# The gates of the last 64 dense tokens kept in SBUF, and eight e-tiles of activations under way in the dense loop

## The chip, the core and the metric

The kernel runs on one core of a Trainium2 chip. The core has a matrix engine (PE, with weight loads shown as PEld), a vector engine (DVE), an activation engine (ACT), GpSimd (POOL) and a queue engine (SP) that issues most transfers. The metric is device time of one execution in microseconds (us), lower is better.

## What is computed

One layer of an encoder block for 512 tokens of width 1024: attention in two branches, then a PEER feed-forward part with 16384 single-neuron experts. The change lies in the PEER part, of which this is the core:

```python
s1 = jnp.einsum('thc,hnc->thn', q[:, :, 0], sub_keys[:, 0])
s2 = jnp.einsum('thc,hnc->thn', q[:, :, 1], sub_keys[:, 1])
...                                   # top 16 of each half, top 16 of the sums
eidx = e1 * PEER_N_KEYS + e2          # 8 heads x 16 experts per token
gate = jax.nn.softmax(top, axis=-1)
act = jax.nn.gelu(jnp.einsum('td,thkd->thk', xc, expert_u[eidx]))
return jnp.einsum('thk,thkd->td', gate * act, expert_v[eidx])
```

## The kernel before

The 512 tokens are split. For 128 of them (block a = 0) the chosen experts are gathered one slot at a time: a job gathers one expert row per token by an indirect transfer on POOL (tile `gat`, 4 buffers, L1058) and DVE reduces it (`gscr`, L1064, for the rows of `expert_u`; `acc`, L1076, for those of `expert_v`). There are 264 jobs, spread by program order over the rest of the kernel.

For the other 384 tokens (ND = 384, blocks DT = 1, 2, 3) the part is computed densely. The experts are 128 e-tiles of 128. For each e-tile:

- `gelu_s` (L870 to L879) loads the tile of `expert_u` (512 KB, tile `raw`), splits it into two float32r parts (`whi` on ACT, L91; `wlo` on DVE, L92), runs 24 matmuls of 384 columns into `pj` (L86 to L88) and writes the Gelu to an `am` tile of 128 x 384. For the first NS = 96 e-tiles this is done ahead (`run_ahead`) and `am` is stored to the DRAM tensor `gls`; for the last 32 it is done in the dense loop. Here "u tile" means one such e-tile.
- The dense loop multiplies `am` by the gates (L1201), splits the product into `ah` and `al`, loads and splits the tile of `expert_v` ("v tile", 512 KB) and runs 18 matmuls of 512 columns into `y` (L1220).

The gates are made dense before the loop, 4 tokens at a time: DVE writes one-hot tiles `oh` (L1125) and `og` (L1130), PE multiplies them into `pg` (L1137), ACT copies `pg` into a `stage` tile that holds 32 tokens (L1139). After each 32 tokens four transfers store the stage to the DRAM tensors `gd` (L1146); there are 12 such groups. In the loop, `gch` (L1164) loads the gates of 8 e-tiles, all 12 groups at once, into one of two buffers.

The e-tiles run in chunks of 8. The order of the chunks is 12, 0, 1, 2, 13, 3, 4, 5, 14, 6, 7, 8, 15, 9, 10, 11; chunks 12 to 15 need `expert_u` in the loop, the others load `am` from `gls`. `stage_s` prepares the e-tile that is LEAD tiles ahead.

What sets the order of the work: a scheduler places each engine's instructions in a fixed order when the kernel is built. Engines run their own order and wait where data or a buffer is missing; SP issues its transfers in order too. The tiles of `expert_u` and `expert_v` share one pool (`w4`, L794): 3 `raw` buffers, 5 `whi` and 5 `wlo`. So the transfer of tile k waits for the split of tile k-3, and the split of tile k for the matmuls of tile k-5.

Of the kernel before, what the change touches and what calls it, by code (L numbers as in the profile page):

```python
# [15 lines left out]
F32 = mybir.dt.float32  # L16
# [6 lines left out]
OP = mybir.AluOpType  # L23
# [872 lines left out]
def peer(K, A, out):  # L896
    nc, cst, gen, Pool = K.nc, K.cst, K.gen, K.Pool
    small, f2, mm3, split, ident = K.small, K.f2, K.mm3, K.split, K.ident
    h2tok = K.h2tok
    gd, gls = A['gd'], A['gls']  # L900
    ND, NS = 384, 96
    RT, OB, SB, J0, GB = 8, 3, 2, 48, 4
    DT = (1, 2, 3)
    pss = Pool("pss", space=PSUM, side="right")
    pe_ = Pool("pse", space=PSUM)
# [1 line left out]
    pa = Pool("am")  # L907

    def pmat():
        return pss.tile([128, 512], F32, name="pj", bufs=2)  # L910
# [4 lines left out]
    def ptr():  # L915
        return pe_.tile([128, 512], F32, name="pt", bufs=2)

    def pg():
        return pe_.tile([128, 512], F32, name="pg", bufs=2)
# [40 lines left out]

    def run_ahead():
        if K.ahead < NS:
            K.run_ahead(pmat(), pa.tile([128, ND], F32, name="am", bufs=4), nc.vector)

    tk = K.wk = Pool("tk")
    wq = A['w_query'].rearrange("(k p) n -> p k n", p=128)
# [54 lines left out]
    def slots(p, a):  # L1021
        rb = ranks(p, a).rearrange("p h f k -> p (h f) k")

        eq = p.tile([128, 16, 16, 16], BF, name="eq", bufs=1)
        for r in range(16):
            nc.vector.scalar_tensor_tensor(eq[:, r], rb, float(r), ib[:, a, :, r, None].to_broadcast([128, 16, 16]),
                                           op0=OP.is_equal, op1=OP.mult)
        ev = eq.rearrange("p r s k -> p r (s k)")
        n = 8
        while n > 1:  # L1030
            nc.vector.tensor_tensor(ev[:, 0:n], ev[:, 0:n], ev[:, n:2 * n], op=OP.add)
            n //= 2
        ef = p.tile([128, 2, 128], F32, name="ef", bufs=2)
        nc.vector.tensor_tensor(ef.rearrange("p f (h k) -> p h f k", k=16), eq[:, 0].rearrange("p (h f) k -> p h f k", f=2),
                                eq[:, 1].rearrange("p (h f) k -> p h f k", f=2), op=OP.add)
        e = [ef[:, f, :] for f in range(2)]
        g = p.tile([128, 8, 16], F32, name="gate", bufs=2)
        nc.vector.tensor_tensor(g, top[:, a], top[:, a, :, 0:1].to_broadcast([128, 8, 16]), op=OP.subtract)
        nc.scalar.activation(g, g, AF.Exp)
        z = small(8)  # L1040
        nc.vector.tensor_reduce(out=z, in_=g, op=OP.add, axis=AX)
        rz = small(8)
        nc.vector.reciprocal(rz, z)
        nc.vector.tensor_tensor(g, g, rz[:, :, None].to_broadcast([128, 8, 16]), op=OP.mult)
        return e[0], e[1], g.rearrange("p h k -> p (h k)")


    g0 = Pool("g0", side="right")
# [38 lines left out]
    def run_jobs(done):  # L1087
        while jobs and njobs - len(jobs) < done:
            jobs.pop(0)()


    gt = K.wk = Pool("gates")
    T = 4

    GS = 16384.0
    iota = gt.tile([128, 128, T], HF, name="iota")
    nc.vector.tensor_copy(iota, ioti[:, :, None].to_broadcast([128, 128, T]))
    e1, e2, g = slots(gt, 0)
    nc.vector.scalar_tensor_tensor(eidx, e1, 128.0, e2, op0=OP.mult, op1=OP.add)
    nc.vector.tensor_copy(gate0, g)  # L1100
    for b, a in enumerate(DT):
        tr = []
        for n, t in enumerate(slots(gt, a)):
            p = ptr()
            nc.tensor.transpose(p[:, :128], t, ident)
            s = gt.tile([128, 128], HF if n < 2 else F32, name=f"sT{n}", bufs=2)
            nc.scalar.activation(s, p[:, :128], AF.Copy, scale=1.0 if n < 2 else GS)
            tr.append(s)
        gT = tr[2]
        gp = []  # L1110
        for i in range(2):
            q = gt.tile([128, 128], HF, name=f"gp{i}", bufs=2)
            nc.vector.tensor_copy(q, gT)
            if i == 0:
                nc.vector.tensor_tensor(gT, gT, q, op=OP.subtract)
            gp.append(q)
        for t0 in range(0, 128, T):
            ts = slice(t0, t0 + T)
            tb = t0 % 32
            if tb == 0:  # L1120
                st = gt.tile([128, 128, 32], F32, name="stage", bufs=SB)
            oh = []
            for i in range(2):
                o = gt.tile([128, 128, T], HF, name=f"oh{i}", bufs=OB)
                nc.vector.tensor_tensor(o, tr[i][:, None, ts].to_broadcast([128, 128, T]), iota, op=OP.is_equal)  # L1125
                oh.append(o)
            pcs = []
            for i in range(2):
                o = gt.tile([128, T, 128], HF, name=f"og{i}", bufs=OB)
                nc.vector.tensor_tensor(  # L1130
                    o, oh[0].rearrange("p e t -> p t e"), gp[i][:, ts, None].to_broadcast([128, T, 128]), op=OP.mult)
                pcs.append(o)
            for q in range(0, T, 4):
                p = pg()
                for j in range(4):
                    for i in range(2):
                        nc.tensor.matmul(p[:, j * 128:j * 128 + 128], oh[1][:, :, q + j], pcs[i][:, q + j, :],  # L1137
                                         start=i == 0, stop=i == 1)
                nc.scalar.activation(st[:, :, tb + q:tb + q + 4].rearrange("p e t -> p t e"),  # L1139
                                     p.rearrange("p (t e) -> p t e", t=4), AF.Copy, scale=1 / GS)  # L1140
            if t0 % 16 == RT:
                run_ahead()
            run_jobs(J0 * (128 * b + t0 + T) // 384)
            if tb == 28:
                for c in range(4):
                    nc.sync.dma_start(gd[c][4 * b + t0 // 32].rearrange("c p e t -> p c (e t)"),  # L1146
                                      st[:, 32 * c:32 * c + 32, :].rearrange("p (c e) t -> p c (e t)", e=8))
    while K.ahead < NS:
        run_ahead()
# [8 lines left out]
    lp = Pool("main")  # L1158
    gch, ams = {}, {}

    def stage_s(e):
        if e % 8 == 0:
            gch[e // 8] = lp.tile([128, 12, 8, 32], F32, name="gch", bufs=2)
            nc.sync.dma_start(gch[e // 8].rearrange("p h e t -> p h (e t)"),  # L1164
                              gd[e // 32][:, e // 8 % 4].rearrange("h p e t -> p h (e t)"))
        am = ams[e] = pa.tile([128, ND], F32, name="am", bufs=4)
        if e < NS:
            nc.sync.dma_start(am, gls[e])
        else:
            gelu_s(e, pmat(), am, nc.vector)  # L1170
# [16 lines left out]
            (nc.scalar if n else nc.sync).dma_start(ov[:, a, ns], y)  # L1187

    PR = (0, 1)
    LEAD = 4  # L1190
    for e in order[:LEAD]:
        stage_s(e)
    pool_order = K.tc.manual_schedule(engines={mybir.EngineType.Pool})
# [2 lines left out]
    for n_, e in enumerate(order):  # L1196
        if n_ + LEAD < 128:
            stage_s(order[n_ + LEAD])
        am = ams.pop(e)
        amv = am.rearrange("p (h t) -> p h t", t=32)  # L1200
        nc.vector.tensor_tensor(amv, amv, gch[e // 8][:, :, e % 8, :], op=OP.mult)  # L1201
        ah = lp.tile([128, ND], F32R, name="ah", bufs=2)
        al = lp.tile([128, ND], F32R, name="al", bufs=2)
        split(ah, al, am)
        raw, vh, vl = w4(v[e])
        split(vh, vl, raw, nc.vector)
        if n_ == 126:
            run_jobs(njobs)
            for a in range(4):
                xr[a] = g0.tile([128, 1024], F32, name="gat", bufs=GB)  # L1210
                nc.sync.dma_start(xr[a], A['x1d'][:, a, :])
            residual(0)
        for b in range(3):
            bs = slice(b * 128, b * 128 + 128)
            prods = [(i, n) for i in range(3) for n in range(2)]
            if n_ == 127:
                prods.sort(key=lambda t: t[1])
            for i, n in prods:
                l, r = ((ah, vh), (ah, vl), (al, vh))[i]
                nc.tensor.matmul(ys[b][n], l[:, bs], r[:, n * 512:n * 512 + 512],  # L1220
                                 start=n_ == 0 and i == 0, stop=n_ == 127 and i == 2)
        done += (njobs - J0) * (1 if e < NS else 2) / (254.0 - NS)
        run_jobs(done)
# [14 lines left out]
def block(tc, A, out):  # L1238
    with ExitStack() as ctx:
        dram = ctx.enter_context(tc.tile_pool(name="dram", bufs=1, space=bass.MemoryType.DRAM))  # L1240
        A['x1d'] = dram.tile([128, 4, 1024], F32, name="x1d")
        A['gd'] = [dram.tile([12, 4, 128, 8, 32], F32, name=f"gd{c}") for c in range(4)]
        A['gls'] = dram.tile([128, 128, 384], F32, name="gls")
        K = Ctx()
        setup(tc, ctx, K)
        front(K, A)
        peer(K, A, out)
# [29 lines left out]
```

## Time and profile before

| what | value |
|---|---|
| median of 3 runs | 2010.34 us (2009.19 to 2011.33) |
| profiled execution | 2011.68 us |
| its span, first to last instruction | 2009.8 us |
| mean granted PE clock | 0.974 of full speed |
| PE busy | 1873.7 us, 93% |
| DVE busy | 1593.2 us, 79% |
| ACT busy | 842.7 us, 42% |
| bytes moved | 447.30 MB |

The span is cut into stretches below: the gates end at about 1314 us, the first matmul of the dense loop starts at 1342.6 us, and the loop ends at about 2000 us.

### The profile page before, as it was taken

The numbers are of one execution on the slowest core, as the hardware profiler recorded it, in microseconds if no ns is written. First come the engines' busy times: TensorE is split into PE (matmuls) and PEld (weight loads), VectorE is DVE, ScalarE is ACT, GpSimd is POOL, SyncE is SP. The second block draws the span as 40 slices with busy tenths as digits, with TensorE's granted clock in tenths as the row PEclk, the third lists the DMA queues.
The fourth block names the chain that finished last, engine by engine and source line by source line (L and its number), as shares of the span: only waits on it lengthen the run. The fifth ranks groups of instructions, "written<-read, shape, count | busy, mean of one in ns | idle before, by whom it ended". The sixth has DMA issues, their size and how long they took to land.

```text
span 2009.8 us, 28332 instructions
## 1 busy us (share of the span) xinstructions
PE 1873.7 (93%) x9858; PEld 1620.1 (81%) x9858; DVE 1593.2 (79%) x3276; ACT 842.7 (42%) x1330; POOL 698.0 (35%) x534
## 2 busy tenths in 40 slices
PE   6999998989899899999989999839999999999998
PEld 5987777778677788899989999828888888878886
DVE  7488585886775759999979989968778888888764
ACT  3444454645633333345545555513333333333342
POOL 2554332352235522012444147233234334323200
PEclk9999999999999999999999999969999999999999
DMA  7334242122256322468688979889999999999962
GB/s 262 86 120 121 63 145 60 35 87 84 59 152 215 128 72 81 147 226 276 229 295 316 322 274 322 299 287 371 360 320 354 342 354 330 355 361 325 345 225 93
DMA packets 206417, 447.30 MB, mean 223 GB/s; under 512 B 17297, under 2 KB 104642, under 8 KB 206146
## 3 DMA queue, kind: packets, MB, share of 16 engines
q1 hardware_dynamic: 168592, 309.14, 45.5%
q0 software_dynamic: 36864, 134.23, 18.8%
q10 hardware_dynamic: 818, 2.12, 0.3%
q8 instruction: 77, 1.26, 0.3%
q14 instruction: 66, 0.54, 0.1%
HBM read 397.20 MB, written 48.23 MB: 222 GB/s over the span
## 4 chain that ended last, share of the span: by engine, by line
PE 51%; DVE 16%; DMA 6%; issue 3%; ACT 2%; POOL 1%; SPq 0%; DVEq 0%; ACTq 0%; POOLq 0%
PE y L1220 26%; PE pj L86 7%; PE pj L87 7%; PE pj L88 7%; DMA raw<-uT 3%; DVE wlo L92 2%; DVE og L1130 2%; PE pg L1137 1%; DVE mr L933 1%; DMA raw<-w_ada 1%; DVE idx L935 1%; ACT whi L91 1%; DMA raw<-expert_v 1%; DVE oh L1125 1%; DVE idx L932 1%
## 5 line engine op out<-in xcount | busy, mean ns | idle before, releaser
L91 ACT ACTIVATE whi<-raw 128x1024 fp32r<-128x1024 f32 (+3 forms) x431 | 382.0, 893 | 382.6 <-PE pj L88 108.5
L92 DVE TENSOR_TENSOR wlo<-raw,whi 128x1024 fp32r<-128x1024 f32 (+3 forms) x339 | 376.9, 1114 | 98.1 <-ACT whi L91 96.7
L86 PE MATMUL pj<-h2h,whi 128*128 128x384 f32 x1008 | 345.8, 343 | 12.0 <-ACT am L879 10.9
L88 PE MATMUL pj<-h2h,wlo 128*128 128x384 f32 x1008 | 344.8, 342 | 5.0 <-DVE wlo L92 5.0
L87 PE MATMUL pj<-h2l,whi 128*128 128x384 f32 x1008 | 345.3, 343 | 0.0
L1058 POOL DMA_INDIRECT gat<-expert_v,eidx x128 | 211.9, 1656 | 316.9 <-DVE acc L1076 219.2
L1058 POOL DMA_INDIRECT gat<-expert_u,eidx x128 | 169.1, 1321 | 401.9 <-DVE gscr L1064 228.2
L1220 PE MATMUL y<-whi,ah 128*128 128x512 f32 x768 | 232.5, 397 | 33.3 <-ACT ah L91 28.4
L1220 PE MATMUL y<-wlo,ah 128*128 128x512 f32 x768 | 243.3, 397 | 0.7 <-DVE wlo L92 0.7
L92 POOL TENSOR_TENSOR wlo<-raw,whi 128x512 fp32r<-128x512 f32 (+2 forms) x92 | 146.5, 1598 | 278.7 <-ACT whi L91 256.0
L1220 PE MATMUL y<-whi,al 128*128 128x512 f32 x768 | 234.5, 395 | 0.0
L91 ACT ACTIVATE ah<-am 128x384 fp32r<-128x384 f32 x128 | 67.0, 524 | 333.5 <-PE y L1220 229.2
L86 PEld LDWEIGHTS pj<-h2h,whi 128*128 128x128 f32 x1008 | 192.2, 191 | 15.7 <-ACT am L879 12.9
L86 PE MATMUL pj<-whi,hh 128*128 128x512 f32 (+2 forms) x512 | 191.7, 387 | 9.8 <-DVE gA L651 4.4
L1220 PEld LDWEIGHTS y<-whi,ah 128*128 128x128 f32 x768 | 144.3, 189 | 67.7 <-ACT ah L91 28.6
L87 PE MATMUL pj<-wlo,hh 128*128 128x512 f32 (+2 forms) x512 | 196.2, 384 | 2.3 <-DVE wlo L92 2.3
L88 PEld LDWEIGHTS pj<-h2h,wlo 128*128 128x128 f32 x1008 | 191.9, 190 | 6.3 <-DVE wlo L92 6.3
L87 PEld LDWEIGHTS pj<-h2l,whi 128*128 128x128 f32 x1008 | 191.8, 190 | 1.1
L88 PE MATMUL pj<-whi,hl 128*128 128x512 f32 (+2 forms) x512 | 191.1, 380 | 0.0
L1220 PEld LDWEIGHTS y<-wlo,ah 128*128 128x128 f32 x768 | 144.7, 188 | 36.1 <-DVE wlo L92 1.2
L1220 PEld LDWEIGHTS y<-whi,al 128*128 128x128 f32 x768 | 144.2, 188 | 35.3
L1076 DVE SCALAR_TENSOR_TENSOR acc<-gat,wts,acc 128x1024 f32<-128x1024 f32 x127 | 162.4, 1279 | 9.6 <-DMA gat<-expert_v,eidx 9.2
(313 smaller groups left out, 3209.5 us busy)
## 6 DMA issues: line engine op xcount, KB each, us to landing
raw<-uT SPq DMA_DIRECT2D x128, 512.0 KB
raw<-expert_v SPq DMA_DIRECT2D x128, 512.0 KB
gd<-stage SPq DMA_DIRECT2D x48, 512.0 KB
gch<-gd SPq DMA_DIRECT2D x16, 1536.0 KB
raw<-w_in SPq DMA_DIRECT2D x88, 256.0 KB
am<-gls SPq DMA_DIRECT2D x96, 192.0 KB
gls<-am SPq DMA_DIRECT2D x94, 192.0 KB
raw<-w_ada SPq DMA_DIRECT2D x64, 256.0 KB
```

The source lines that it names most:

```text
L86: nc.tensor.matmul(ps, lh, rh, start=start, stop=False)
L87: nc.tensor.matmul(ps, lh, rl, start=False, stop=False)
L88: nc.tensor.matmul(ps, ll, rh, start=False, stop=stop)
L91: nc.scalar.activation(hi, raw, AF.Copy)
L92: (eng or nc.vector).tensor_tensor(lo, raw, hi.bitcast(F32), op=OP.subtract)
L932: nc.vector.max_index(out=i[:, 0:8], in_max=v[:, 0:8], in_values=s)
L933: nc.vector.match_replace(out=r, in_to_replace=v[:, 0:8], in_values=s, imm_value=-3.0e38)
L935: nc.vector.max_index(out=i[:, 8:16], in_max=v[:, 8:16], in_values=r)
L1058: nc.gpsimd.indirect_dma_start(out=t, out_offset=None, in_=src, in_offset=bass.IndirectOffsetOnAxis(ap=eidx[:, s:s + 1], axis=0))
L1076: nc.vector.scalar_tensor_tensor(acc, t, wts[:, s:s + 1], acc, op0=OP.mult, op1=OP.add)
L1130: nc.vector.tensor_tensor(o, oh[0].rearrange("p e t -> p t e"), gp[i][:, ts, None].to_broadcast([128, T, 128]), op=OP.mult)
L1220: nc.tensor.matmul(ys[b][n], l[:, bs], r[:, n * 512:n * 512 + 512], start=n_ == 0 and i == 0, stop=n_ == 127 and i == 2)
```

## The change

The stage becomes one tile `stg` of two halves, taken from a pool that lives to the end of the kernel. Groups 0 to 9 are stored to `gd` as before; groups 10 and 11 (64 tokens) are not, they stay in the two halves. `gd` and `gch` shrink from 12 to 10 groups. The multiplication of `am` by the gates becomes two instructions: 320 columns from `gch` and 64 columns from `stg`. `am` has 8 buffers instead of 4, in the loop and in `run_ahead`, and LEAD is 8 instead of 4. The slots of block 0 are computed ahead of the `iota` tile.

```diff
-            K.run_ahead(pmat(), pa.tile([128, ND], F32, name="am", bufs=4), nc.vector)
+            K.run_ahead(pmat(), pa.tile([128, ND], F32, name="am", bufs=8), nc.vector)
...
+    stg = g0.tile([128, 2, 128, 32], F32, name="stage")
...
+    e1, e2, g = slots(gt, 0)
     iota = gt.tile([128, 128, T], HF, name="iota")
     nc.vector.tensor_copy(iota, ioti[:, :, None].to_broadcast([128, 128, T]))
-    e1, e2, g = slots(gt, 0)
...
-            if tb == 0:
-                st = gt.tile([128, 128, 32], F32, name="stage", bufs=SB)
+            grp = 4 * b + t0 // 32
+            st = stg[:, grp % 2]
...
-            if tb == 28:
+            if tb == 28 and grp < 10:
...
-            gch[e // 8] = lp.tile([128, 12, 8, 32], F32, name="gch", bufs=2)
+            gch[e // 8] = lp.tile([128, 10, 8, 32], F32, name="gch", bufs=2)
...
-        am = ams[e] = pa.tile([128, ND], F32, name="am", bufs=4)
+        am = ams[e] = pa.tile([128, ND], F32, name="am", bufs=8)
...
-    LEAD = 4
+    LEAD = 8
...
-        nc.vector.tensor_tensor(amv, amv, gch[e // 8][:, :, e % 8, :], op=OP.mult)
+        nc.vector.tensor_tensor(amv[:, :10], amv[:, :10], gch[e // 8][:, :, e % 8, :], op=OP.mult)
+        nc.vector.tensor_tensor(amv[:, 10:], amv[:, 10:], stg[:, :, e, :], op=OP.mult)
...
-        A['gd'] = [dram.tile([12, 4, 128, 8, 32], F32, name=f"gd{c}") for c in range(4)]
+        A['gd'] = [dram.tile([10, 4, 128, 8, 32], F32, name=f"gd{c}") for c in range(4)]
```

SP's order at the end of the gates. Before, the last two groups and then the first two loads of gates, with `expert_v` tiles between:

```order
L1146 DMA gd_58<-stage 128x4x256
L1146 DMA gd_59<-stage 128x4x256
L1146 DMA gd_60<-stage 128x4x256
L1146 DMA gd_61<-stage 128x4x256
L799 DMA raw<-expert_v 128x1024 x2
L1146 DMA gd_58<-stage 128x4x256
L1146 DMA gd_59<-stage 128x4x256
L1146 DMA gd_60<-stage 128x4x256
L1146 DMA gd_61<-stage 128x4x256
L1164 DMA gch<-gd_61 128x12x256
L1164 DMA gch<-gd_58 128x12x256
```

Now (the `gd` rows here are group 9, the last that is stored):

```order
L1148 DMA gd_61<-stage 128x4x256
L799 DMA raw<-uT 128x1024
L883 DMA gls<-am 128x384
L799 DMA raw<-uT 128x1024
L883 DMA gls<-am 128x384
L799 DMA raw<-uT 128x1024 x2
L799 DMA raw<-expert_v 128x1024 x8
L1166 DMA gch<-gd_61 128x10x256
L1166 DMA gch<-gd_58 128x10x256 x2
L1170 DMA am<-gls 128x384 x3
```

Eight stores are gone, eight v tiles stand ahead of the first load of gates, and no store stands between.

DVE's order over the last groups of gates. Before, no split (L92) stands there; `oh`, `og` are the one-hot tiles, `gscr` a job:

```order
L1125 TENSOR_TENSOR oh_10960<-sT_10147,iota 128x512
L1130 TENSOR_TENSOR og_10941<-oh_10937,gp_10153 128x512
L1130 TENSOR_TENSOR og_10943<-oh_10937,gp_10156 128x512
L1064 SCALAR_TENSOR_TENSOR gscr,act<-gat,h2tok 128x1024
L1130 TENSOR_TENSOR og_10962<-oh_10958,gp_10153 128x512
L1130 TENSOR_TENSOR og_10964<-oh_10958,gp_10156 128x512
L1125 TENSOR_TENSOR oh_10976<-sT_10143,iota 128x512
```

Now, at the same place:

```order
L1064 SCALAR_TENSOR_TENSOR gscr,act<-gat,h2tok 128x1024
L1127 TENSOR_TENSOR oh_10945<-sT_10140,iota 128x512
L1132 TENSOR_TENSOR og_10947<-oh_10943,gp_10146 128x512
L1132 TENSOR_TENSOR og_10949<-oh_10943,gp_10149 128x512
L92 TENSOR_TENSOR wlo<-raw,whi 128x1024
L1127 TENSOR_TENSOR oh_10961<-sT_10136,iota 128x512
L1127 TENSOR_TENSOR oh_10982<-sT_10136,iota 128x512
L1127 TENSOR_TENSOR oh_10963<-sT_10140,iota 128x512
L1064 SCALAR_TENSOR_TENSOR gscr,act<-gat,h2tok 128x1024
L1127 TENSOR_TENSOR oh_10984<-sT_10140,iota 128x512
L92 TENSOR_TENSOR wlo<-raw,whi 128x1024
```

Two more splits stand inside the gates: those of v tiles 3 and 4 (counted from 0).

DVE's order from the last gates into the loop. Before:

```order
L1130 TENSOR_TENSOR og_11053<-oh_11049,gp_10153 128x512
L1130 TENSOR_TENSOR og_11055<-oh_11049,gp_10156 128x512
L1064 SCALAR_TENSOR_TENSOR gscr,act<-gat,h2tok 128x1024 x4
L1069 TENSOR_TENSOR wts<-wts,gate_8064 128x16
L1076 SCALAR_TENSOR_TENSOR acc<-gat,wts,acc 128x1024 x5
L1201 TENSOR_TENSOR am<-am,gch 128x384 x4
```

Now:

```order
L1132 TENSOR_TENSOR og_11038<-oh_11034,gp_10146 128x512
L1132 TENSOR_TENSOR og_11040<-oh_11034,gp_10149 128x512
L1064 SCALAR_TENSOR_TENSOR gscr,act<-gat,h2tok 128x1024 x2
L1204 TENSOR_TENSOR am<-am,stage 128x64 x8
L1064 SCALAR_TENSOR_TENSOR gscr,act<-gat,h2tok 128x1024 x2
L1203 TENSOR_TENSOR am<-am,gch 128x320 x8
L1069 TENSOR_TENSOR wts<-wts,gate_8064 128x16
L92 TENSOR_TENSOR al<-am,ah 128x384 x2
```

The five `acc` jobs ahead of the first multiplication are gone from there, and eight e-tiles are multiplied in a row.

On PE and ACT, all eight u tiles of chunk 12 now have their matmuls and their Gelu ahead of the first `ah` of the loop; before, two of them had both behind it, and two more the Gelu.

Ahead of these places each engine's order is as it was, but for the `iota` row and two neighbours on DVE.

## Rows read from the trace of the kernel before

**Rows 1.** The page: the span, the busy time of each engine, and the 40 slices of 50.2 us (tenths; PEclk is the granted PE clock, DMA the busy share of the 16 DMA engines).

```profile
span 2009.8 us, 28332 instructions
PE 1873.7 (93%) x9858; PEld 1620.1 (81%) x9858; DVE 1593.2 (79%) x3276; ACT 842.7 (42%) x1330; POOL 698.0 (35%) x534
...
PE   6999998989899899999989999839999999999998
...
PEclk9999999999999999999999999969999999999999
DMA  7334242122256322468688979889999999999962
```

**Rows 2.** PE in order of time around the end of the gates and the first e-tiles: start, us, instruction, count, and in brackets the idle time before it and who ended it. The rows at 1352.84 and 1356.90 are the first and the last of 24 matmuls of one u tile, those at 1361.28 and 1365.27 of the next.

```profile
1313.32 0.91 PE L1137 MATMUL pg<-og,oh 128*128 128x128 f16 x7 [0.30 <-DVE og L1130]
1342.61 1.22 PE L1220 MATMUL y<-whi,ah 128*128 128x512 f32 x2 [28.38 <-ACT ah L91]
...
1352.84 0.34 PE L86 MATMUL pj<-h2h,whi 128*128 128x384 f32 x1
...
1356.90 0.34 PE L88 MATMUL pj<-h2h,wlo 128*128 128x384 f32 x1
...
1361.28 0.34 PE L86 MATMUL pj<-h2h,whi 128*128 128x384 f32 x1
...
1365.27 0.34 PE L88 MATMUL pj<-h2h,wlo 128*128 128x384 f32 x1
```

**Rows 3.** The chain of waits that ended last, in order of time, across the same gap: start, us, what.

```profile
1315.35 0.38 SPq L1146
...
1317.40 11.76 DMA gd<-stage
1329.30 11.99 DMA gch<-gd
1341.34 0.04 issue
1341.39 0.57 DVE am L1201
...
1342.03 0.53 ACT ah L91
```

**Rows 4.** SP's issues in order of time over the last groups of gates.

```profile
1262.53 3.21 SPq L1146 DMA_DIRECT2D gd<-stage  x4
...
1292.35 0.33 SPq L799 DMA_DIRECT2D raw<-expert_v  x1
1297.84 3.16 SPq L1146 DMA_DIRECT2D gd<-stage  x4
1301.10 3.36 SPq L799 DMA_DIRECT2D raw<-expert_v  x2
```

**Rows 5.** DVE in order of time over the last gates: the last split, the last `og` pair, and the first `acc` job behind them.

```profile
1300.20 1.21 DVE L92 TENSOR_TENSOR wlo<-raw,whi 128x1024 fp32r<-128x1024 f32 x1
1301.33 0.41 DVE L1125 TENSOR_TENSOR oh<-sT,iota 128x512 f16<-128x512 f16 x1
...
1311.98 1.28 DVE L1130 TENSOR_TENSOR og<-oh,gp 128x512 f16<-128x512 f16 x2
1313.19 1.21 DVE L1064 SCALAR_TENSOR_TENSOR gscr<-gat,h2tok 128x1024 bf16<-128x1024 f32 x1
...
1322.53 1.28 DVE L1076 SCALAR_TENSOR_TENSOR acc<-gat,wts,acc 128x1024 f32<-128x1024 f32 x1 [3.86 <-DMA gat<-expert_v,eidx]
```

**Rows 6.** POOL in order of time: the gather that the last row above waits for.

```profile
1314.68 1.80 POOL L1058 DMA_INDIRECT gat<-expert_v,eidx  x1 [1.20 <-DVE gscr L1064]
```

**Rows 7.** Busy time by stretch: bounds and length, then busy us and count of PE, PEld, DVE, ACT, POOL, then the granted PE clock, the DMA share and GB/s.

```profile
1283.00:1315.00 32.00, 21.52 (x160) 17.91 (x159) 31.97 (x58) 18.14 (x20) 7.68 (x8) 0.80 0.79 261
1315.00:1330.00 15.00, 0.00 (x0) 0.00 (x0) 8.46 (x11) 0.54 (x2) 7.16 (x7) 0.50 1.01 358
1330.00:1343.00 13.00, 0.40 (x1) 0.40 (x2) 2.90 (x5) 0.94 (x2) 1.87 (x2) 0.50 1.04 357
...
1357.00:1392.00 35.00, 35.00 (x158) 29.02 (x157) 28.54 (x38) 12.39 (x17) 15.18 (x13) 1.00 1.00 364
1392.00:1426.00 34.00, 34.00 (x147) 27.34 (x147) 27.12 (x42) 11.32 (x16) 9.53 (x10) 1.00 1.01 372
...
1357.00:1910.00 553.00, 545.35 (x2474) 457.35 (x2472) 449.69 (x586) 189.92 (x260) 202.14 (x165) 1.00 0.96 347
```

**Rows 8.** Waits of PE from 1342 us to the end: who waited for whom, us in total, times, longest.

```profile
PE y L1220 <- ACT ah L91: 28.4, 1, 28.4
PE y L1220 <- ACT whi L91: 4.9, 4, 1.5
PE pj L86 <- ACT whi L91: 1.1, 1, 1.1
PE pj L88 <- DVE wlo L92: 0.9, 2, 0.6
PE y L1220 <- DVE wlo L92: 0.7, 1, 0.7
```

**Rows 9.** DVE's groups from 1342 to 2000 us, shapes kept apart: count, busy us, mean ns, idle before.

```profile
L92 DVE TENSOR_TENSOR wlo<-raw,whi 128x1024 fp32r<-128x1024 f32 x149 | 181.9, 1221 | 19.5 <-ACT whi L91 18.4 <-issue 0.8
L1201 DVE TENSOR_TENSOR am<-am,gch 128x384 f32<-128x384 f32 x127 | 69.6, 554 | 36.5 <-DMA am<-gls 27.2 <-ACT am L879 8.7
```

**Rows 10.** Waits of SP in the loop, from 1342 to 1990 us, and of ACT from 870 to 1315 us.

```profile
SPq L1164 <- DVE am L1201: 15.3, 12, 3.4
...
ACT am L879 <- issue: 16.3, 6, 3.1
```

More of the change, by code (lines that the diff above doesn't have):

```diff
@@ L901, in peer @@
     ND, NS = 384, 96
-    RT, OB, SB, J0, GB = 8, 3, 2, 48, 4
+    RT, OB, J0, GB = 8, 3, 48, 4
     DT = (1, 2, 3)
@@ L1143, in peer @@
             run_jobs(J0 * (128 * b + t0 + T) // 384)
-            if tb == 28:
+            if tb == 28 and grp < 10:
                 for c in range(4):
-                    nc.sync.dma_start(gd[c][4 * b + t0 // 32].rearrange("c p e t -> p c (e t)"),
+                    nc.sync.dma_start(gd[c][grp].rearrange("c p e t -> p c (e t)"),
                                       st[:, 32 * c:32 * c + 32, :].rearrange("p (c e) t -> p c (e t)", e=8))
```

## The prediction, on record before the change was run

> **What bounds the kernel now.** I read the page first [rows 1]: PE is busy 93% of the span, at full clock in every slice but one. That slice, the 27th of the 40, shows PE at 3 tenths and the granted clock at 6, while the DMA digit is 8. So PE sets the time nearly everywhere, and there is one hole. PE in order of time [rows 2] gives its size: the last matmul of the gates starts at 1313.32, the first of the dense loop at 1342.61, and 28.38 us of idle stand between. The chain of waits [rows 3] says what fills the hole: the last stage is stored (issue at 1315.35 to 1317.40, 11.76 us to land), only then can the first load of gates go (1329.30, 11.99 us), then one multiplication and one `ah`. It is a round trip through DRAM, behind the last group of gates.
>
> The loop behind it is a PE stage: its waits of PE sum to 36.0 us, of which 28.4 are the hole [rows 8], so 7.6 us are left in some 650 us. But it has company close behind: the DMA share is 0.96 from 1357 to 1910 us at 347 GB/s, and 1.00 to 1.01 in the first 69 us at 364 to 372 GB/s [rows 7].
>
> **What the change does to the hole.** The groups that the first load of gates needs now end with group 9, whose stores are issued at 1262.53 [rows 4]; with the 11.76 us of [rows 3] they land before 1280. The store is off the path. The load is not simply early, though: SP's order puts it behind eight v tiles, and v tile 7 gets its `raw` buffer only when v tile 4 is split. So I follow DVE.
>
> 1. The split at 1300.20 to 1301.33 [rows 5] is the last before the gates end; in the new order v tile 2 stands there. From it to the end of the last `og` DVE needs 1313.19 - 1301.33 = 11.9 us, without a wait. The new order adds the splits of v tiles 3 and 4 there. A split costs 1.13 us in a row of work (1300.20 to 1301.33).
> 2. The split of v tile 4 needs the `whi` and `wlo` buffers of u tile 7, so the matmuls of that tile. PE has two u tiles more to do here, 8.4 us: the first and the last of 24 matmuls stand 4.06 us apart in the one and 3.99 in the other [rows 2], and 24/23 of that is 4.24 and 4.16. PE is busy 21.5 of the 32 us from 1283 to 1315 [rows 7], so it has 10.5 us of room, most of it after 1297; the last of the two should end near 1307. DVE meets this with about 1 us of wait. I place the split of v tile 4 at 1311 and the last `og` at 1313.2 + 2.3 + 1 = 1316.5.
> 3. The load of gates is issued behind v tile 7, near 1311.6. Nothing in the rows shows a load of 10 groups; the old one of 12, issued with a second beside it and with gathers in flight, took 11.99 us. A sixth less in bytes and one v tile ahead of it about cancel: I take 12.0, so 1323.6. Bounds: 10 us by bytes alone (10/12 of 11.99), 16 us if the v tiles ahead hold it back by a third.
> 4. DVE must be there too. Behind the last `og` stand four jobs and eight multiplications of 64 columns. The last of these jobs waits for a gather issued when the third job back frees its buffer, at about 1315.7; the gather issued at 1314.68 was read at 1322.53, 7.85 us later [rows 5, 6]. By that the last job starts at 1323.5 and ends at 1324.7. This is a little later than the load, so the multiplications start at 1324.7.
> 5. From the first multiplication to the first matmul it was 1342.61 - 1341.39 = 1.22 us [rows 2, 3]. The loop starts at 1325.9, not 1342.6: **16.7 us** earlier. Some 8 us of hole are left, and with it the low clock.
>
> **What else moves.** The two u tiles whose matmuls stood inside the loop [rows 2] are now done in holes of the gates: **8.4 us** of PE work less behind the start.
>
> The split multiplication adds 128 DVE instructions. No row shows one of 320 or 64 columns. From the two shapes that are shown [rows 9], 1221 ns for 1024 columns and 554 for 384, the slope is 1.04 ns a column and the fixed part 154 ns. So each e-tile costs about 0.154 us more, 19.7 us over the loop. DVE is busy 450 of the 553 us from 1357 to 1910 [rows 7], and 36.5 us of idle stand before the old multiplication [rows 9]; 19.7 us fit there, PE covers them, and I cost them at 0. If that cover were gone they would cost all 19.7.
>
> `am` with 8 buffers and LEAD 8 give each load of `am` four more e-tiles of 4.2 us; the 27.2 us for which DVE waited for `am` [rows 9] should shrink. PE did not pay for them, so 0; at most the 7.6 us of waits in the loop go with them. Ahead of the gates' end, ACT waited 16.3 us for what looks like a free `am` [rows 10]; PE was full there for the most part, so 0, with a gain of up to 4 us as a bound.
>
> Bytes: two groups less are stored and loaded. A store is 4 x 512 KB, so 4.2 MB less written, and the 16 loads shrink from 1536 to 1280 KB, 4.2 MB less read. Under PE cover this is worth 0 in time; it is room for the DMA, since the loop wants the same work in 8.4 us less.
>
> **The sum.** 16.7 + 8.4 = 25.1 us less. Of the profiled execution's own 2011.7 us that leaves 1986.6; it lies 1.3 us above the median of the runs, so I forecast **1985 us** for the median.
>
> The vector page speaks against the change. The Trainium skill (VectorE: DVE Perf Modes, section The TRN2 errata) says that each SBUF instruction pays a fixed latency, so many small ones pay it often, and asks for tiles of 512 elements and more; by its formula for float32 the pair would cost, as an estimate, about 0.16 us more than the single one. The rows give the same fixed part, but they also say that PE waits for DVE in 0.7 and 0.9 us of the loop [rows 8], so the price is not on the path. By the rule taken as time, the sum would be 20 us worse, which is the third rival below.
>
> **Rivals.**
>
> - *The hole shrinks less.* If the matmuls of u tile 7 or the transfer of v tile 4 come later than I have them, the split of v tile 4 slides to the end of the gates and the load goes out at 1316.5, not 1311.6. With 12 us it lands at 1328.5, and the loop starts at 1329.7: 1989 us. For it: eight transfers in a row through three buffers. Against: the DMA share is 0.79 from 1283 to 1315 [rows 7], with 2.1 MB of stores at 1297.84 that now go away [rows 4].
> - *The DMA bounds the loop.* If the transfers of the first 550 us are the limit, an earlier PE only waits more. The end then moves by the bytes saved from 1315 on: 14 loads of gates times 0.262 MB and one group of 2.1 MB, 5.8 MB at 364 GB/s, 16 us: 1994 us. For it: the share of 0.96. Against: PE was full from 1357 to 1426 at 364 to 372 GB/s. The Trainium skill (DMA: Bandwidth & Descriptors, Specifications) sets the limit of a core at about 358 GB/s; the rows read 372 over 34 us, so the measurement decides and there is more room than by that figure.
> - *DVE shows.* All 19.7 us of the added instructions on the path: 2005 us. For it: DVE is in order, and `wlo` and `al` stand behind the multiplications. Against: 36.5 us of idle before them.
> - *Slower: SP's queue blocks.* A load of gates waits until the last multiplication of the chunk two back frees its buffer, and the v tiles stand behind it in SP's order. Before, these waits were 15.3 us in 12, 3.4 at most, and cost PE nothing [rows 10]. If each of the 13 later loads now held the v tiles so long that PE stood 3.4 us, that would be 44 us: 2029 us. It decides from 25.1 / 13 = 1.9 us a chunk on. Against: with LEAD 8 a load of gates is prepared eight e-tiles ahead of its use and not four.
>
> **How the numbers follow.** The forecast's own case (1979 to 1988) has a chance of 0.58, a smaller hole (1988 to 1992) 0.13, the DMA 0.13, DVE 0.07, a result within 4 us of before, by several small losses, 0.04, the blocked queue or another loss of its size 0.05. The range reaches down by the 7.6 us of loop waits (1977) and up over the DMA case and the upper bound of the load, 16 us, together with some of DVE's price (2001); this leaves out about 0.16. This kernel's measurement tells about 0.2%, 4 us, from no change. Faster by that takes the first four cases, 0.91; within 0.2% 0.04; slower 0.05.
>
> **What would show it.** Right: no stores for the last two groups, the first `gch` issued near 1312 and landed near 1324, the hole of PE 8 to 9 us, the loop's start near 1326 with no u tile in its first eight e-tiles, PE's waits in the loop still under 10 us, DVE's busy time up by some 20 us. Wrong: a hole of 12 us and more (the load is late: look at when v tile 4 is split), waits of PE for `whi` or `wlo` in the loop that end on a transfer of `expert_v` or on DVE, or a DMA share of 1.00 with PE idle.

## The result, and the profile after

The changed kernel takes **1984.3 us** (median of six runs, 1982.8 to 1992.7), the kernel before 2010.8 beside it: a ratio of 0.9872, 95% interval 0.9851 to 0.9893. The forecast was 1985 us. Its profiled execution took 1986.2 us. The page of it, beside [rows 1]:

```profile
span 1984.4 us, 28322 instructions
...
PE 1870.2 (94%) x9858; PEld 1616.9 (81%) x9858; DVE 1597.2 (80%) x3404; ACT 841.6 (42%) x1330; POOL 709.6 (36%) x534
...
PE   6989998989899899899999999979999999999998
...
PEclk9999999999999999999989999979999999999999
DMA  7334242122146422368769888989989999999982
```

PE has almost the same work, 1870.2 us and not 1873.7. The slice with the hole reads 7 and not 3. The waits of PE from 1320 us on, which answer to [rows 8]:

```profile
PE y L1223 <- ACT ah L91: 8.5, 1, 8.5
PE y L1223 <- ACT whi L91: 2.2, 2, 1.1
PE y L1223 <- DVE wlo L92: 1.7, 2, 0.8
PE pj L86 <- ACT whi L91: 1.1, 1, 1.1
PE pj L88 <- DVE wlo L92: 0.6, 1, 0.6
```

The hole went from 28.4 to 8.5 us, the other waits from 7.6 to 5.6. The chain that ended last, across the gap [rows 3]:

```profile
1314.32 4.58 issue
...
1319.13 8.05 DMA gat<-expert_u,eidx
...
1327.27 1.23 DVE gscr L1064 x2
1328.50 0.41 DVE am L1203
...
1328.94 0.53 ACT ah L91
...
1329.52 15.53 PE y L1223 x56
```

No store and no load of gates stands in it any more. A gather of a token-row job does, as in step 4 of the prediction. The first load of gates was issued at 1315.1, and SP, which waits for it ahead of its third load, went on at 1325.1, before that gather landed. The loop starts at 1329.5, 13.1 us earlier than before, not 16.7; and from there to the end it is 12.3 us shorter (1329.5 to 1984.4 is 654.9 us; 1342.6 to 2009.8 was 667.2), not 8.4. Of the 12.3, 8.4 are the two u tiles (48 matmuls less behind the start) and 2.0 the shorter waits; the last 1.9 were not traced. The sum came out; its terms did not. DVE in order of time shows the first part [rows 5]:

```profile
1309.75 1.21 DVE L92 TENSOR_TENSOR wlo<-raw,whi 128x1024 fp32r<-128x1024 f32 x1
...
1313.38 1.26 DVE L92 TENSOR_TENSOR wlo<-raw,whi 128x1024 fp32r<-128x1024 f32 x1
...
1318.78 1.28 DVE L1132 TENSOR_TENSOR og<-oh,gp 128x512 f16<-128x512 f16 x2
...
1322.39 1.17 DVE L1204 TENSOR_TENSOR am<-am,stage 128x64 f32<-128x64 f32 x8
...
1327.27 1.22 DVE L1064 SCALAR_TENSOR_TENSOR gscr<-gat,h2tok 128x1024 bf16<-128x1024 f32 x1 [2.57 <-DMA gat<-expert_u,eidx]
...
1328.42 3.30 DVE L1203 TENSOR_TENSOR am<-am,gch 128x320 f32<-128x320 f32 x8
```

The two added splits are there. The last `og` ends at 1320.0, where the prediction had 1316.5. From then on it goes by the prediction: 1319.4, the start of the last `og`, to the first y matmul are 10.1 us. DVE's groups of the loop [rows 9]:

```profile
L1203 DVE TENSOR_TENSOR am<-am,gch 128x320 f32<-128x320 f32 x128 | 61.6, 486 | 16.5 <-ACT am L879 11.1 <-DMA am<-gls 5.1
L1204 DVE TENSOR_TENSOR am<-am,stage 128x64 f32<-128x64 f32 x128 | 27.2, 218 | 0.0
```

486 and 218 ns are 704 for 554 before, 150 ns more an e-tile, 19.2 us in all, if the recorded durations are added up. But these overlap: in a row, the next instruction starts before the recorded end of the one ahead of it. The eight multiplications of 64 columns above took 1.17 us together, where eight times 218 ns are 1.74, and the eight of 320 columns 3.30 us; before, four of 384 columns took 1.96 us:

```profile
1341.39 1.96 DVE L1201 TENSOR_TENSOR am<-am,gch 128x384 f32<-128x384 f32 x4 [9.58 <-DMA gch<-gd]
```

From start to start (the length of the row less its last duration, by the number of steps) that is 136, 402 and 469 ns, so the pair takes some 69 ns more of DVE's time, 8.8 us in all and not 19.2. DVE's busy time on the page, which counts overlaps once, rose by 4.0 us only (1593.2 to 1597.2), and by 10.6 from 1357 to 1910 us (449.7 to 460.3). The wait for `am` fell from 27.2 to 5.1 us.

### The profile page after: what moved, and what is told of

Same layout as the page of the kernel before. It is cut to its first block, busy times and chain, and to the rows that moved or that the text cites. A ratio compares the mean times of both kernels' runs of the same rounds, so it can differ in the third digit from the quotient of the medians.

```text
span 1984.4 us, 28322 instructions
## 1 busy us (share of the span) xinstructions
PE 1870.2 (94%) x9858; PEld 1616.9 (81%) x9858; DVE 1597.2 (80%) x3404; ACT 841.6 (42%) x1330; POOL 709.6 (36%) x534
## 4 chain that ended last, share of the span: by engine, by line
PE 44%; DVE 14%; issue 10%; POOL 5%; DMA 4%; ACT 1%; SPq 0%; DVEq 0%; POOLq 0%; ACTq 0%
PE y L1223 27%; PE pj L86 5%; PE pj L87 5%; PE pj L88 4%; POOL gat L1058 4%; DVE wlo L92 2%; DMA raw<-w_ada 1%; DMA raw<-uT 1%; DMA gat<-expert_u,eidx 1%; DVE mr L933 1%; DVE idx L935 1%; DVE idx L932 1%; DVE cand L952 1%; DVE vals L934 1%; DVE vals L931 1%
## 5 line engine op out<-in xcount | busy, mean ns | idle before, releaser
L92 DVE TENSOR_TENSOR wlo<-raw,whi 128x1024 fp32r<-128x1024 f32 (+3 forms) x339 | 375.9, 1110 | 98.6 <-ACT whi L91 97.8
L1058 POOL DMA_INDIRECT gat<-expert_v,eidx x128 | 219.0, 1711 | 301.4 <-DVE acc L1076 206.1
L92 POOL TENSOR_TENSOR wlo<-raw,whi 128x512 fp32r<-128x512 f32 (+2 forms) x92 | 147.4, 1608 | 278.1 <-ACT whi L91 255.5
```

The lines of the kernel that those rows point to most:

```text
L92: (eng or nc.vector).tensor_tensor(lo, raw, hi.bitcast(F32), op=OP.subtract)
L1058: nc.gpsimd.indirect_dma_start(out=t, out_offset=None, in_=src, in_offset=bass.IndirectOffsetOnAxis(ap=eidx[:, s:s + 1], axis=0))
```

## The experiments

Three lengths of each profiled execution order what follows: from the first to the last `og` on DVE (the gates), from the last `og` to the first y matmul (the gap), and from there to the end. The rows for four kernels, instruction groups with their first and last start (the kernel before, the changed one, the gates alone on chip, and one of the arrangements below; each pair is `og`, then `y`):

```profile
L1130 DVE TENSOR_TENSOR og<-oh,gp x192: 632/681/736, 921.4 to 1312.6; 128x512 f16<-128x512 f16 x192
L1220 PE MATMUL y<-whi,ah x8: 392/578/794, 1342.6 to 1348.9; 128*128 128x512 f32 x8
```

```profile
L1132 DVE TENSOR_TENSOR og<-oh,gp x192: 630/679/736, 920.0 to 1319.4; 128x512 f16<-128x512 f16 x192
L1223 PE MATMUL y<-whi,ah x28: 392/394/794, 1329.5 to 1349.8; 128*128 128x512 f32 x28
```

```profile
L1132 DVE TENSOR_TENSOR og<-oh,gp x192: 634/680/739, 919.2 to 1311.8; 128x512 f16<-128x512 f16 x192
L1223 PE MATMUL y<-whi,ah x30: 392/396/794, 1319.7 to 1349.6; 128*128 128x512 f32 x30
```

```profile
L1134 DVE TENSOR_TENSOR og<-oh,gp x192: 637/681/734, 915.9 to 1293.9; 128x512 f16<-128x512 f16 x192
L1223 PE MATMUL y<-whi,ah x58: 392/394/628, 1308.3 to 1349.4; 128*128 128x512 f32 x58
```

Worked out so for all (jobs: `gscr` and `acc` instructions that stand ahead of the first multiplication in DVE's program order, where the 66 of the code count two `weigh` too; us). The gates, the gap and the rest come from one execution each, the median from all. The medians were taken at different times, with the kernel before at 2010.8 to 2012.8 beside them, so compare kernels by the ratio. The gap is no idle time by itself: in c1, d3, c2 and b2 PE does u tiles in it, and in c2 and b2 three u tiles more than in the changed kernel, in d3 one, are left for the rest.

| kernel | jobs | gates | gap | rest | median | ratio to before, 95% |
|---|---|---|---|---|---|---|
| before | 85 | 391.2 | 30.0 | 667.2 | 2010.8 | |
| changed | 78 | 399.4 | 10.1 | 654.9 | 1984.3 | 0.9872 (0.9851 to 0.9893) |
| a3, same program | 78 | 396.9 | 10.1 | 655.5 | 1984.0 | 0.9851 (0.9821 to 0.9882) |
| a1, gates alone | 78 | 396.0 | 9.1 | 663.7 | 1991.4 | 0.9882 (0.9836 to 0.9928) |
| d1, the same | 78 | 392.6 | 7.9 | 662.8 | 1985.4 | 0.9872 (0.9847 to 0.9896) |
| a2, lead alone | 85 | 391.7 | 30.7 | 662.8 | 2008.2 | 0.9985 (0.9966 to 1.0004) |
| a4, load on POOL | 78 | 396.1 | 11.4 | 652.3 | 1982.2 | 0.9845 (0.9817 to 0.9872) |
| c1, 66 jobs | 64 | 378.0 | 14.4 | 654.3 | 1965.7 | 0.9771 (0.9756 to 0.9785) |
| d3, 58 jobs | 56 | 362.3 | 22.1 | 657.0 | 1969.8 | 0.9784 (0.9760 to 0.9808) |
| c2, 44 jobs | 44 | 340.2 | 33.8 | 675.2 | 1972.1 | 0.9795 (0.9781 to 0.9808) |
| d4, before, 66 jobs | 64 | 375.2 | 23.8 | 674.7 | 1997.3 | 0.9919 (0.9895 to 0.9942) |
| b2, more DVE | 47 | 349.7 | 27.6 | 672.1 | 1968.7 | 0.9780 (0.9765 to 0.9795) |
| b3, more DMA, SP | 78 | 398.8 | 10.1 | 661.9 | 1992.1 | 0.9901 (0.9885 to 0.9916) |
| d2, more DMA, ACT | 78 | 392.3 | 10.3 | 661.0 | 1986.2 | 0.9872 (0.9848 to 0.9896) |

**a3 turned into a repeat.** The edit spreads the 48 jobs over fewer tokens.

```diff
-            run_jobs(J0 * (128 * b + t0 + T) // 384)
+            run_jobs(min(J0, J0 * (128 * b + t0 + T) // 352))
```

> The changed kernel with its 48 jobs spread over the first 352 of the 384 gate tokens, not over all, so that no gather job stands ahead of the first multiplications. If the last job's gather held the start (as the chain says) and the gate load landed at 1325.1: start near 1326.2, 3.3 us earlier, 1981 us (1980 to 1982.5). Rival, the load of the gates landed only just before 1328.4, with the gather: no gain, 1984.

The program came out with the same instructions in the same order on every engine: what places a job is the scheduler, not the line of code that it is written on. So 1984.0 (1979.6 to 1989.7) is the changed kernel again, and tells nothing on the gather. The five executions with the same order on DVE and PE up to the gap (changed, a3, a4, b3, d2) give the scatter of the gates: 399.4, 396.9, 396.1, 398.8 and 392.3. One part of it can be seen in the changed kernel's own execution, where PE stood 4.1 us near 1190 and ACT's splits ahead of it had waited longer for transfers of uT (waits of PE and ACT from 1140 to 1200 us, and a stretch with columns as in [rows 7]; then the same of d2, where PE did not wait):

```profile
PE pj L86 <- ACT am L879: 4.1, 1, 4.1
```

```profile
ACT whi L91 <- DMA raw<-uT: 17.8, 6, 7.4
```

```profile
1180.00:1200.00 20.00, 15.90 (x103) 14.72 (x102) 14.19 (x23) 9.82 (x12) 8.60 (x4) 0.91 0.78 271
```

```profile
ACT whi L91 <- DMA raw<-uT: 9.4, 4, 2.8
```

```profile
1180.00:1200.00 20.00, 20.00 (x146) 19.05 (x146) 17.73 (x27) 12.47 (x15) 11.33 (x3) 1.00 0.83 290
```

**The two parts apart: a1 and d1** (the gates on chip, lead four) **and a2** (the lead alone).

```diff
 a1 and d1, from the changed kernel         a2, from the kernel before
-    LEAD = 8                               -    LEAD = 4
+    LEAD = 4                               +    LEAD = 8
-  name="am", bufs=8                        -  name="am", bufs=4
+  name="am", bufs=4                        +  name="am", bufs=8
```

> The gates of the last 64 tokens stay on chip, the lead stays at four e-tiles with four am buffers. If the two parts add up (the load's wait for the last gate columns is worth the 13.1 us by which the first y matmul of the changed kernel started earlier, the lead is worth the 8.4 us of u tiles): 1996.5 us, 1994 to 1999, first y matmul near 1329.5, hole of PE near 17 us (8.5 and the 8.4 of four u tiles that are now behind it), no shorter loop. Rival, the lead is what counts (deeper loads, fewer waits): 2005 or more. Rival, either part alone gives nearly all: under 1990.

> The kernel before with a lead of eight e-tiles and eight am buffers; all twelve groups of gates still go through memory. If the parts add up: 2001 us, 1999 to 2003: first y matmul still near 1342.6, hole near 20 us (28.4 less 8.4), loop 8.4 us shorter by the u tiles, perhaps 2 more by waits. Rival, the lead is what counts: 1990 or less. Rival, the u tiles were no cost in the loop: 2010.

> The kernel with the gates on chip and a lead of four once more, with more rounds, since its four times spread over 16 us: what is the deeper lead worth on top of it? If the two u tiles more save their 8.4 us in the loop and cost nothing ahead of it: 1992.7 us. If they cost VectorE two splits (2.4 us) ahead of the start: 1990. If they cost as much ahead as the spans of the two profiles say (start 4.5 us later): 1988.5.

The gates alone missed their 1996.5: 1991.4 in a1, with runs from 1978.8 to 1994.8, and 1985.4 in d1, the same program, which is faster than all three numbers named for it. The lead alone missed its 2001 and came out at 2008.2, nearest to its rival of 2010.

Both ways the lead is worth less than 8.4 us. On top of the gates it gives 2.4 us (means of the ten runs of a1 and d1 and of the ten of the changed program, 1987.5 and 1985.2; some 4 us uncertain). Alone it gives 3.0 us by the ratio, between -0.8 and 6.8, so 8.4 lies outside. The gates alone give 25.8 us by d1 (20.9 to 30.8) and 23.7 by a1 (14.5 to 33.0). The table says where: on top of the gates the lead does make the rest 8.0 us shorter (663.2, the mean of a1 and d1, to 655.2), but the gap is 1.6 us longer (8.5 to 10.1), and two more splits of 1.2 us stand on DVE ahead of it (79 between the first and the last `og`, for 77). The u tiles were not taken into an empty hole; part of their price was moved ahead of the start. Alone, the lead makes the rest only 4.4 us shorter: PE's waits behind the start are 11.2 us there, for 7.6 before. The gates take the gap from 30.0 to 8.5, and the rest from 667.2 to 663.2.

**The load of gates issued from POOL: a4.** (The other edit is that of a3 and has no effect.)

```diff
-            nc.sync.dma_start(gch[e // 8]...
+            (nc.gpsimd if e == NS else nc.sync).dma_start(gch[e // 8]...
```

> As the one with the jobs spread over 352 tokens, and the first load of gate columns is issued from GpSimd's queue behind its 48 jobs, not from SyncE's behind eight loads of v. If what then ends last is the last gate copy at 1322.1 and its two multiplications: start near 1324.5, 1979.5 us. Rival, GpSimd issues it no earlier, or the load takes longer from there: as the one before or slower, 1981 to 1986.

It missed its 1979.5 and came out as the rival had it: 1982.2 us, not told apart from the changed kernel. The chain now ends on this load, since POOL issues it behind the same gathers:

```profile
1313.45 4.59 issue
...
1319.42 9.34 DMA gch<-gd
1328.78 0.50 DVE am L1203
```

**Fewer jobs ahead of the start: c1, c2, d3, and d4 on the kernel before.** POOL's queue is held in the written order from the gates on, so that the load on it is a barrier that the later gathers cannot pass.

```diff
-    RT, OB, J0, GB = 8, 3, 48, 4
+    RT, OB, J0, GB = 8, 3, 66, 4        (44 in c2, 58 in d3)
+    pool_order = K.tc.manual_schedule(engines={mybir.EngineType.Pool})
+    pool_order.__enter__()              (moved ahead of the loop over DT)
+            (nc.gpsimd if e == NS else nc.sync).dma_start(gch[e // 8]...
```

> The changed kernel with GpSimd's queue held in the order in which the program is written from the gates on, 66 token-row jobs before the loop (in the changed kernel 78 of them stand before the first multiplication on VectorE), and the first load of gate columns on GpSimd's queue behind them. If the start is held by VectorE's work and by what stands ahead of that load: 12 jobs less are 15 us of VectorE work less, the load lands before the last gate copy, the start is that copy plus 2.4 us, between 1319 and 1325, and the loop grows by 0 to 3 us: 1976 to 1983. Rival, TensorE's own work holds the start, or the jobs cost in the loop what they gave back: 1984 or more.

> As the one with 66 jobs, with 44. 34 jobs less before the start are 43 us of VectorE work; the start should then be held by TensorE, near 1319, and the loop takes 34 gathers more, 17 MB or 47 us of transfers on top of a DMA share of 0.89. If TensorE still covers them: 1975 to 1979. Rival, the loop becomes bound by its transfers: 1985 to 2000.

> As the one with 66 jobs before the loop, with 58. With 66 TensorE still waited 3.3 us at the start and ended last; with 44 it waited for nothing there, but the last gathers of the jobs ended some 13 us behind TensorE. In between, if eight jobs of 1.27 us are what the start still lacks and the jobs stay inside the loop: 1961 to 1964 us. Rival, the jobs end last already: 1966 to 1969.

> The kernel before (all twelve groups through memory, lead four) with the same 66 jobs and the first load on GpSimd's queue. If VectorE's work holds the end of the gates in the kernel before too, the gates end about 15 us earlier but the store and the load still follow: 1993 to 1999 us, hole still near 28 us or more; the changed kernel with 66 jobs is then 27 to 33 us faster, more than the 26 us of the change itself. Rival, the jobs moved into the loop only fill the hole less: 2005 to 2011.

The gates get shorter with what is taken off DVE. Between the first and the last `og` stand 66 of the 78 jobs and 79 splits in the changed kernel, 54 and 76 in c1; at 1.3 and 1.2 us each that is 19 us less, and c1's gates are 14 to 21 us shorter than those of the changed program. So DVE's jobs largely set when the last `og` comes. It does not follow that PE stood still so much longer: it is busy for 384 of the 399 us of that stretch. What the earlier `og` saves PE is its waits at the end. c1 beats both kernels by far, 1965.7 us, lower than was expected (1976 to 1983), and its loop starts at 1308.3, not between 1319 and 1325. Its waits of PE from 1280 on:

```profile
PE y L1223 <- ACT ah L91: 3.3, 1, 3.3
PE y L1223 <- ACT whi L91: 2.6, 3, 1.1
PE pj L86 <- ACT whi L91: 1.1, 1, 1.1
PE y L1223 <- DVE wlo L92: 1.0, 2, 0.8
```

With 0.6 us more for another `wlo` that is 8.6 us, for 20.1 in the changed kernel, of which 4.7 were waits for `og`; c1 has none of these. Besides, the same 9858 matmuls keep PE busy for 1864.3 us, not 1870.2: from 1283 to 1350 us the granted clock was 0.97 of full speed in c1 and 0.85 in the changed kernel (means over its two levels). Both together are 17.4 of the 21.8 us between the spans of the two profiles. The three edits of c1 come together, and holding POOL's order was not tried by itself; but the load on POOL alone gave nothing clear (a4), and b2 below, with neither, gets most of the gain with fewer jobs, though DVE work is added in it.

c2 missed both its ranges, with 1972.1. PE waits 5.5 us in it, but the jobs moved into the loop end behind it. PE's last matmul ends at 1956.2, and it is not the bytes, as its rival had it, but the last gathers that hold the end:

```profile
1947.37 1.86 POOL gat L1058
...
1949.54 8.36 DMA gat<-expert_v,eidx
...
1957.99 1.30 DVE acc L1076
```

d3, with 58 jobs, missed its 1961 to 1964: 1969.8 us, not told apart from 66 jobs (the intervals overlap). d4 came as expected in its time, 1997.3 us, but its hole is 20.1 us and not 28. The kernel before gains from fewer jobs too, and in this arrangement the change is worth 31.7 us by the medians (1997.3 to 1965.7) and some 30 by the ratios (24 to 35), which is not told apart from its own 26.5.

**More work for DVE: b2.**

```diff
+        nc.vector.tensor_tensor(scr[:, :ND], am, am, op=OP.mult)
```

> The changed kernel with one more VectorE multiplication of 128x384 in each of the 128 e-tiles, into a scratch tile that nobody reads: about 557 ns a tile, 71 us of VectorE work more, against the 19.2 us that the split multiplication added. If VectorE's added work lies beside TensorE's: 1984 to 1988 us, TensorE's waits in the loop still under 12 us. Rival, the added VectorE work is exposed tile by tile: 2055 us; half exposed, 2020.

It got faster, 1968.7 us, which no theory had. Only 47 jobs stand ahead of the start in its program, most likely because the scheduler saw a longer loop, so b2 is another c2. From 1300 to 1960 the added group, and PE's waits from 1320 on:

```profile
L1205 DVE TENSOR_TENSOR gscr<-am 128x384 bf16<-128x384 f32 x125 | 68.8, 550 | 0.3
```

```profile
PE y L1224 <- ACT ah L91: 1.3, 1, 1.3
PE y L1224 <- ACT whi L91: 1.1, 1, 1.1
PE pj L86 <- ACT am L879: 1.0, 1, 1.0
PE y L1224 <- DVE wlo L92: 0.7, 1, 0.7
PE y L1224 <- DVE al L92: 0.3, 1, 0.3
```

69 us more of DVE in the loop by durations (DVE's busy time on the page is 59.9 us more), and 31 jobs more, leave PE 4.4 us of waits. Its jobs end behind PE, as in c2, which has no added work and is no faster. So the much smaller price of the split multiplication lies beside PE's work.

**The bytes: b3 and d2.** The loads read again what the change no longer reads, from SP's queue and from ACT's.

```diff
+            more = lp.tile([128, 2, 8, 32], F32, name="more", bufs=1)
+            nc.sync.dma_start(more...,      (nc.scalar in d2)
+                              gd[e // 32][0:2, e // 8 % 4]...)
```

> The changed kernel, and with each of the 16 loads of gate columns a second load of 256 KB from the same buffer into a tile that nobody reads (yo has five buffers, not six, to make room): the 4.2 MB that the change no longer reads are read again, some 11.5 us of transfers at the 364 GB/s of the loop. If the loop's bytes are worth nothing under TensorE's cover: 1984 to 1987 us. Rival, the loop got shorter because it moves less: 1990 to 1996.

> The changed kernel with the same 4.2 MB of loads more, issued from ScalarE's queue, not SyncE's: if it was the bytes that cost 8 us, 1990 to 1994 again. If it was the order of SyncE's queue, where each of these loads stands ahead of loads of am and v: 1984 to 1987.

By their medians the two contradict each other: 7.9 us more from SP's queue, as the rival of b3 had it, and 1.9 from ACT's (5.8 and 0.0 by the ratios), which would say that it was the order of SP's queue. The profiles don't bear that out: both have a rest that is 6 to 7 us longer than that of the changed program, and both the same new waits of PE from 1335 on. These two lines read alike in b3 and in d2; the first was 2.2 us in the changed kernel, and the second is not there from 1335 on:

```profile
PE y L1226 <- ACT whi L91: 5.0, 5, 1.5
PE pj L88 <- DVE wlo L92: 1.7, 3, 0.6
```

What d2 gained back it gained ahead of the gap (gates 392.3), where its program is that of the changed kernel. So the loop is not indifferent to 4.2 MB, but how much of it reaches the time, and whether the bytes do it or the new order around them (DVE's and PE's order differ from 1341 us on), stays open.

## Why the prediction was right

The mechanism was right: the round trip left the path, and the gates kept on chip bring nearly all of the gain. That the median lies within 1 us of the forecast is luck, for the start came 3.6 us later than forecast and the rest 3.9 us shorter, and these cancel.

- *The round trip leaves the path.* Right. From the start of the last `og` to the first y matmul it forecast 10.0 us, and 10.1 came. The last job's gather ended last, as in step 4, not the load.
- *The gates end 3.3 us later (steps 1 and 2).* Too small: 6.8 us in this execution. This is why the start moved by 13.1 us and not by 16.7. The two splits are there. By its length the stretch is 8.2 us longer here than before, and 1.1 to 7.6 in the others of the same order; one late transfer is shown above, the rest of the scatter was not traced. The first rival, a smaller hole, came near in its place of the start (1329.7), but not by its mechanism: the load was issued at 1315.1, not 1316.5, and the chain runs through the gather.
- *Two u tiles, 8.4 us.* The rest did get 8.0 us shorter, yet the lead brings 2 to 3 us, since splits and matmuls of these tiles now stand ahead of the start. The prediction had counted this, 3.3 us, but as a later end of the gates. Netted, it gave the lead 5.1 us and the gates 20.0. By the runs it is 2 to 3 for the lead (up to 6.8) and 24 to 26 for the gates (d1: 20.9 to 30.8), so it had the gates some 4 to 6 us too low, at the edge of what the runs can tell, and the lead is not told apart from 5.1.
- *Waits of the loop and bytes, 0.* Too low. PE's waits fell by 2.0 us, and with the gates alone the rest is 4.0 us shorter than before without any u tile moved. Less traffic is the likely cause: b3 and d2, which read 4.2 MB more, have a rest 6 to 7 us longer. They do not settle it. The rival in which the DMA bounds the loop gave 1994 us and did not come; the start's gain was kept.
- *DVE's price at 0.* Right in the time. Its size was not: 150 ns an e-tile by durations, for the 154 of the estimate, but 69 ns from start to start. The sign that was named for it, DVE's busy time up by some 20 us, did not come: it rose by 4.0. The prediction had taken a split at 1.13 us from start to start in step 1, and the price of the pair from durations. The Trainium skill (VectorE: DVE Perf Modes, section The TRN2 errata) lets each small instruction pay its fixed latency: the durations agree with its formula (0.15 us more for the estimate of 0.16), and the time from start to start shows under half of that.
- *The blocked queue.* It did not come: SP's loads of gates waited 18.8 us in 12 for the multiplications, 15.3 before, but PE's waits in the loop fell.

## What to carry to other kernels

A load that waits for a store of the same data is a whole round trip; keeping only the last pieces on chip takes it off the path, at the price of one more small instruction a tile. Work that is moved out of a bounded loop must be followed to the place where it lands: here its splits went to DVE ahead of the start, and of 8.4 us some 2 to 3 were left. Durations in a trace can overlap, so the price of one more small instruction is read from start to start, in a row of them. And where a scheduler places filler work, look at what it put ahead of the barrier: with 14 jobs fewer there, POOL's order held and the first load on its queue, the kernel was another 18.6 us faster.

## What the runs showed that was not expected

- The same program differs by up to 13 us between executions (1979.6 to 1992.7). The stretch of the gates alone differs by 7.1 us between executions alike up to there (392.3 to 399.4), but it is not all: a3's profiled execution is 3.5 us longer than the changed kernel's with gates that are 2.5 us shorter, because its first `og` starts 5.4 us later.
- The gather of `expert_u` on the chain took 8.05 us to land, beside the two loads of gates; the five such gathers from 1295 to 1345 us had a median of 5.0. The gather at the same place took 8.0 in b3 and 8.2 in d2, but 5.4 in d1.
- Where no hole is left, the loop starts at full clock. The first y matmuls take up to 794 ns in the changed kernel, whose granted clock was 0.50, the lower level, from 1315 to 1330 us, in which PE was busy for 3.9; in c2, at 1.00 from 1283 to 1330, with PE busy throughout, none up to 1349 us takes more than 400:

```profile
L1223 PE MATMUL y<-whi,ah x60: 390/396/400, 1296.4 to 1348.8; 128*128 128x512 f32 x60
```
